# Two sides of raw-weight homes in the down projection of a hybrid decoder layer

## The chip, the core and the metric

One core of one Trainium2 chip runs the whole layer in one launch. The metric is the device time of one execution, in microseconds (us). Before the change three runs gave 1212.75, 1213.9 and 1214.02, a median of 1213.9.

## What is computed

The reference is one decoder layer on 256 tokens behind 16 meta tokens, in float32, cut here to its outline:

```python
def hybrid_layer(h, ...):
    u = rmsnorm(h, norm_mix)
    proj = u @ w_in                                    # 2048 -> 7176
    ret = head_norm(retention(q_r, k_r, v_r)) * silu(g_r)      # 8 heads
    hm = head_norm(mlstm(q_m, k_m, v_m, i, f)) * sigmoid(o_m)  # 4 heads
    h = h + concat(ret, hm) @ w_out                    # 2048 -> 2048
    u = rmsnorm(h, norm_ffn)
    gate, val = split(causal_dwconv(u @ w_up, width 3))        # 2048 -> 2 x 5632
    return h + (silu(gate) * val) @ w_down             # 5632 -> 2048
out = rmsnorm(hybrid_layer(...), norm_final)[:, 16:]
```

The change concerns the last product, `w_down`, and the memory into which all weights are loaded.

## The kernel before

**Products.** Every float32 weight block is split into a high part `whi` (ScalarE copy to fp32r, L121 or L744) and a low part `wlo` (VectorE subtraction, L123 or L746), and TensorE adds three products: high times high, high times low, low times high. A weight block is 128 x 1024 floats, 512 KB. It lands in a raw home `wraw`; there are four such homes (L116, `bufs=4`), taken in turn. The split parts have five buffers each. A raw home is free again when both halves of the split have read it.

**The stages.** Input projection and heads, output projection, then twice (for `half` in 0 and 1) 22 pairs of up-projection tiles followed by the down projection of those 22 x 256 rows. In each half the down projection runs over two pairs of column blocks (`b` = 0 and 2, L897), and in each pair over eleven steps q = 0 to 10. In half 0 the up projection ends and the down projection begins at about 720 us of the span, its second pair at about 779 us, and the up projection of half 1 at about 833 us; half 1's down projection begins at about 1089 us.

**Plain steps** (q = 0, 4, 9, 10; L919 to 924) load two blocks through `load_w`, split each and make 24 products of 128 x 512.

**Sums steps** (q = 1, 2, 3, 5, 6, 7, 8; `seven`, L812) replace the eight block products by seven of sums of blocks, 21 products of 128 x 512 in all. A step needs three raw blocks (768 KB, L821) and a fourth that was combined before and put away in DRAM, the kept piece (256 KB, L820). They lie in one of two places `left[0]` and `left[1]`, used in turn. VectorE then makes two tiles of differences, `ta` (128 x 1024, L824) and `tb` (128 x 512, L825), which take two of the four raw homes, and four splits follow: two of the raw blocks (called `hT` in the profile), `ta` and `tb`. So VectorE has per sums step four operations of 1024 columns and two of 512.

**Kept pieces** are made during the up projection (`Early`, L704). GpSimd loads raw blocks into a free place (L715), VectorE combines them (L720, L721), GpSimd writes the result to DRAM (L722). In half 0 the last two of these use `left[0]` and `left[1]`, so the first sums step's own loads into `left` wait for them: the 768 KB for L721, the kept piece (L820) for the write of L722 to end.

**The order of the work.** A scheduler of the framework orders each engine's instructions when the program is built. All plain loads, kept pieces and 768 KB loads are issued by SP, in one order; a load whose home is not free holds up the loads behind it. In half 0's first pair the homes go: step 0 takes two, steps 1, 2 and 3 take two each for `ta` and `tb`, and step 4's loads wait for the split of step 2's `ta` and `tb`.

Of the kernel before, what the change touches and what calls it, by code (L numbers as in the profile page):

```python
# [10 lines left out]
F32 = mybir.dt.float32  # L11
# [5 lines left out]
P = 128  # L17
# [16 lines left out]
W0 = GW + 2 * P  # L34
# [49 lines left out]
def trunk(ctx: ExitStack, tc: tile.TileContext, io, out: bass.AP):  # L84
    nc = tc.nc
# [5 lines left out]
    wpool = ctx.enter_context(pool("wpool", 1, side="left"))  # L91
# [20 lines left out]

    last_load = None

    def load_w(src, shape, to=None):
        nonlocal last_load  # L116
        raw = wpool.tile(shape, F32, name="wraw", bufs=4)
        last_load = nc.sync.dma_start(raw, src)
        to, n = (wpool, 5) if to in (None, wpool) else (to, None)
        hi = to.tile(shape, F32R, name="whi", bufs=n)  # L120
        nc.scalar.copy(hi, raw)  # L121
        lo = to.tile(shape, F32R, name="wlo", bufs=n)
        nc.vector.tensor_tensor(out=lo, in0=raw, in1=hi.bitcast(F32), op=ALU.subtract)  # L123
        return hi, lo
# [81 lines left out]
    with pool("sq", 1, side="right") as sqp:  # L206
        for k0, k1 in [(0, 1), (1, 2)] + [(k, k + 2) for k in range(2, KT, 2)]:
            n = k1 - k0
            nc.sync.dma_start(hT[:, k0:k1, :], io["xT"][:, k0:k1, :])
            if k0 == 0:  # L210
                nc.sync.dma_start(par[:, 0:KT], io["par"][:, 0:KT])
            raw = wpool.tile([P, 2, W0], F32, name="wraw", bufs=4)[:, :n, :]

            queue = nc.scalar if k0 < 2 else nc.sync
            load = queue.dma_start(raw, io["w0"][:, k0:k1, :])
            if k0 >= 2:
                last_load = load
# [476 lines left out]
    NQD = NHF // 2  # L694
# [29 lines left out]
    for half in range(2):  # L724
# [24 lines left out]
        for jj in range(NHF):  # L749
            j = half * NHF + jj  # L750
# [61 lines left out]
        def seven(b, q, cs, ps, first, last, after, norm):  # L812
# [8 lines left out]
            nc.sync.dma_start(raw[:, 1:4, :], io["wd7"][b // 2, half * NQD + q][:, 1:4, :])  # L821
            ta, tb = (wpool.tile([P, 2, 512], F32, name="wraw", bufs=4) for _ in range(2))

# [66 lines left out]

        def load_step(b, q, to=wpool):
            return load_w(io["wd"][b, half * NQD + q], [P, 2, 512], to)

# [3 lines left out]
        for b in (0, 2):  # L897
# [10 lines left out]
            alone = plain[-lag:] if final else []  # L908
            for q in steps:
                if q in fast:  # L910
# [8 lines left out]
                for j in range(2):  # L919
                    if j == 1 and q in alone:  # L920
                        continue
                    w = load_step(b + j, q)
                    for tt in range(2):
                        product(cs[tt, j], tt, q, w, q == plain[0], q == plain[-1 - (lag if final and (tt, j) == (1, 1) else 0)])
# [16 lines left out]
        if half == 1:  # L941
            c = 3 * 512
            ws = {}
            for n, q in enumerate(alone):
                ws[q] = load_step(3, q, more if n % 2 else wpool)
                product(cs[0, 1], 0, q, ws[q], False, q == alone[-1])
# [102 lines left out]
```

## Time and profile before

| | |
|---|---|
| median of three runs | 1213.9 us |
| the profiled execution's own time | 1212.13 us |
| its span, first to last instruction | 1210.4 us |
| TensorE busy | 1198.6 us (99%) |
| VectorE busy | 970.1 us (80%) |
| ScalarE busy | 708.5 us (59%) |
| granted TensorE clock, mean | 0.998 |
| DMA, mean over the span | 218 GB/s |

The profile covers one execution. What lies outside its span is 1.73 us. A product of 128 x 512 is shown as 0.39 us long, but the products overlap: the time of a run of them is the distance between their starts. "Idle before" in a row is the engine's idle time just ahead of the instruction, with what ended it.

### The profile page before, as it was taken

What the parts mean: (1) busy time and instruction counts of PE and PEld (TensorE: products, weight loads), DVE (VectorE), ACT (ScalarE), POOL (GpSimd) and SP (SyncE); (2) the same over time, 40 slices, a digit from 0 to 9 for tenths busy, and PEclk for the clock granted to TensorE, in tenths of its full rate; (3) what the DMA queues carried; (4) which work ended last, traced back from release to release, by engine and by line L of the source; (5) the groups of instructions that cost most, each with busy time, mean ns of one, the idle gap of its engine ahead of it and who ended that gap; (6) DMA issues with size and microseconds to landing.
All of it is one profiled execution on the core that took longest, in us unless ns stands there. A gap on an engine that the chain in (4) does not pass through costs nothing.

```text
span 1210.4 us, 22758 instructions
## 1 busy us (share of the span) xinstructions
PE 1198.6 (99%) x8956; PEld 1155.6 (95%) x8956; DVE 970.1 (80%) x1444; ACT 708.5 (59%) x963; POOL 165.1 (14%) x228
## 2 busy tenths in 40 slices
PE   9999999999999999999999999999999999999997
PEld 9999999999999999999999997788999999998886
DVE  8877778766775767789888879996798778789897
ACT  8657646656556656555555546665555555556674
POOL 0100001111110211021122210202022112100232
PEclk9999999999999999999999999999999999999999
DMA  8765555656564655766766775959777677755956
GB/s 277 265 220 160 166 189 171 199 175 189 181 193 141 208 178 176 248 220 208 246 225 209 270 268 202 261 200 272 275 252 261 216 245 239 259 177 208 286 179 185
DMA packets 83004, 263.27 MB, mean 218 GB/s; under 512 B 14672, under 2 KB 18896, under 8 KB 82768
## 3 DMA queue, kind: packets, MB, share of 16 engines
q1 hardware_dynamic: 71952, 223.85, 56.4%
q0 software_dynamic: 10368, 37.11, 10.0%
q8 instruction: 70, 1.15, 0.4%
q10 hardware_dynamic: 576, 0.85, 0.2%
q14 instruction: 38, 0.31, 0.1%
HBM read 243.42 MB, written 11.27 MB: 210 GB/s over the span
## 4 chain that ended last, share of the span: by engine, by line
PE 92%; DMA 4%; DVE 2%; issue 1%; ACT 0%; SPq 0%; DVEq 0%; POOL 0%; ACTq 0%; POOLq 0%
PE mmps L130 25%; PE mmps L131 25%; PE mmps L133 24%; PE atps L807 3%; PE atps L808 3%; PE atps L810 2%; PE mmps L842 2%; PE mmps L839 1%; PE mmps L840 1%; PE atps L842 1%; PE atps L840 1%; PE atps L839 1%; DMA wraw<-in_wd 1%; DMA hT<-in_wd 1%; DVE wlo L746 1%
## 5 line engine op out<-in xcount | busy, mean ns | idle before, releaser
L121 ACT CAST whi<-wraw 128x1024 fp32r<-128x1024 f32 x352 | 368.7, 1049 | 316.6 <-PE mmps L131 216.9
L123 DVE TENSOR_TENSOR wlo<-wraw,whi 128x1024 fp32r<-128x1024 f32 x352 | 433.1, 1232 | 71.9 <-ACT whi L121 69.6
L130 PE MATMUL mmps<-uh,whi 128*128 128x258 f32 x1408 | 346.7, 283 | 0.0
L131 PE MATMUL mmps<-ul,whi 128*128 128x258 f32 x1408 | 346.6, 283 | 0.0
L131 PEld LDWEIGHTS mmps<-ul,whi 128*128 128x128 f32 x1408 | 266.6, 189 | 0.1
L130 PEld LDWEIGHTS mmps<-uh,whi 128*128 128x128 f32 x1408 | 266.4, 189 | 0.1
L130 PE MATMUL mmps<-xh,whi 128*128 128x272 f32 (+2 forms) x864 | 219.9, 288 | 0.0
L131 PE MATMUL mmps<-xl,whi 128*128 128x272 f32 (+2 forms) x864 | 218.4, 286 | 0.0
L133 PE MATMUL mmps<-uh,wlo 128*128 128x258 f32 x1408 | 199.0, 283 | 0.0
L133 PEld LDWEIGHTS mmps<-uh,wlo 128*128 128x128 f32 x1408 | 181.3, 189 | 0.0
L131 PEld LDWEIGHTS mmps<-xl,whi 128*128 128x128 f32 x864 | 163.0, 189 | 0.0
L130 PEld LDWEIGHTS mmps<-xh,whi 128*128 128x128 f32 x864 | 162.7, 188 | 0.1
L133 PE MATMUL mmps<-xh,wlo 128*128 128x272 f32 (+2 forms) x864 | 126.8, 286 | 0.0
L133 PEld LDWEIGHTS mmps<-xh,wlo 128*128 128x128 f32 x864 | 114.4, 188 | 0.0
L633 DVE TENSOR_TENSOR cu<-mmps,rstd 128x258 f32<-128x258 f32 x88 | 37.3, 424 | 47.6 <-PE mmps L133 47.1
L746 DVE TENSOR_TENSOR wlo<-hT,whi 128x1024 fp32r<-128x1024 f32 x52 | 62.8, 1236 | 5.6 <-ACT whi L744 5.0
L744 ACT CAST whi<-hT 128x1024 fp32r<-128x1024 f32 x52 | 53.3, 1051 | 23.4 <-DMA hT<-in_wd 5.6
L131 PE MATMUL mmps<-mixl,whi 128*128 128x258 f32 x256 | 63.0, 283 | 0.0
L130 PE MATMUL mmps<-mixh,whi 128*128 128x258 f32 x256 | 62.4, 283 | 0.0
L744 ACT CAST whi<-wraw 128x1024 fp32r<-128x1024 f32 (+1 forms) x52 | 42.1, 835 | 18.5 <-DVE wraw L824 4.8
L807 PE MATMUL atps<-whi,mh 128*128 128x512 f32 (+1 forms) x132 | 50.9, 387 | 2.0 <-ACT whi L121 2.0
L746 DVE TENSOR_TENSOR wlo<-wraw,whi 128x1024 fp32r<-128x1024 f32 (+1 forms) x52 | 51.4, 1014 | 0.8 <-PE mmps L842 0.2
(276 smaller groups left out, 1704.4 us busy)
## 6 DMA issues: line engine op xcount, KB each, us to landing
wraw<-in_wu SPq DMA_DIRECT2D x176, 512.0 KB, 4.4
wraw<-in_wi SPq DMA_DIRECT2D x108, 512.0 KB, 4.2
hT<-in_wd SPq DMA_DIRECT2D x26, 768.0 KB, 4.5
wraw<-in_wd SPq DMA_DIRECT2D x36, 512.0 KB, 5.1
wraw<-in_wo SPq DMA_DIRECT2D x32, 512.0 KB, 3.8
x<-in_wd POOLq DMA_DIRECT2D x14, 768.0 KB, 7.6
hT<-in_wd POOLq DMA_DIRECT2D x12, 768.0 KB, 6.4
hn<-x POOLq DMA_DIRECT2D x27, 256.0 KB, 7.8
```

The lines of the kernel that those rows point to most:

```text
L121: nc.scalar.copy(hi, raw)
L123: nc.vector.tensor_tensor(out=lo, in0=raw, in1=hi.bitcast(F32), op=ALU.subtract)
L130: nc.tensor.matmul(ps, hi[:, k, :], xh(kk), start=kk == first, stop=False)
L131: nc.tensor.matmul(ps, hi[:, k, :], xl(kk), start=False, stop=False)
L133: nc.tensor.matmul(ps, lo[:, k, :], xh(kk), start=False, stop=kk == last)
L633: evacuated = nc.vector.tensor_tensor(out=u, in0=ps[:, :NQ], in1=rstd2, op=ALU.mult)
L744: copied = nc.scalar.copy(hi, x)
L746: return copied, nc.vector.tensor_tensor(out=lo, in0=x, in1=hi.bitcast(F32), op=ALU.subtract)
L807: nc.tensor.matmul(ps, ah[i], hi[:, i, cols], start=first and i == 0, stop=False)
L808: nc.tensor.matmul(ps, al[i], hi[:, i, cols], start=False, stop=False)
L810: nc.tensor.matmul(ps, ah[i], lo[:, i, cols], start=False, stop=last and i == 1)
L842: nc.tensor.matmul(o, sh[:, f, m, :], lo[:, i, :], start=False, stop=end)
```

## The change

The four raw homes become two sides of two, `wraw0` and `wraw1`, of the same total size. Loads outside the down projection take them in the order 0, 0, 1, 1. In the down projection `ta` and `tb` of a sums step take side 1, and plain steps take side 0, except the last one of a pair (q = 10, and of half 1's second pair the one where the index is odd), which takes side 1. The loads of a plain step that follows a sums step are asked for ahead of that sums step; the splits stay where they were. Nothing is computed otherwise.

```diff
     last_load = None
+    loads = 0
+
+    def raw_home(shape, side):
+        return wpool.tile(shape, F32, name=f"wraw{side}", bufs=2)
+
+    def load_raw(src, shape, side=None):
+
+        nonlocal last_load, loads
+        raw = raw_home(shape, loads % 4 // 2 if side is None else side)
+        loads += 1
+        last_load = nc.sync.dma_start(raw, src)
+        return raw
 
     def load_w(src, shape, to=None):
-        nonlocal last_load
-        raw = wpool.tile(shape, F32, name="wraw", bufs=4)
-        last_load = nc.sync.dma_start(raw, src)
+        return split_w(load_raw(src, shape), shape, to)
+
+    def split_w(raw, shape, to=None):
...
-            ta, tb = (wpool.tile([P, 2, 512], F32, name="wraw", bufs=4) for _ in range(2))
+            ta, tb = (raw_home([P, 2, 512], 1) for _ in range(2))
...
-        def load_step(b, q, to=wpool):
-            return load_w(io["wd"][b, half * NQD + q], [P, 2, 512], to)
+        def load_step(b, q, side):
+
+            return load_raw(io["wd"][b, half * NQD + q], [P, 2, 512], side)
+
+        def split_step(raw, to=wpool):
+            return split_w(raw, [P, 2, 512], to)
...
-            for q in steps:
+            raws = {}
+
+            def load_plain(q):
+                side = 0 if q == plain[0] or q not in steps[steps.index(fast[-1]) + 2 :] else plain.index(q) % 2
+                for j in range(1 if q in alone else 2):
+                    raws[q, j] = load_step(b + j, q, side)
+
+            for n, q in enumerate(steps):
+
+                if q in plain and (q, 0) not in raws:
+                    load_plain(q)
+                if n + 1 < len(steps) and steps[n + 1] in plain and q in fast:
+                    load_plain(steps[n + 1])
                 if q in fast:
...
-                    w = load_step(b + j, q)
+                    w = split_step(raws[q, j])
...
-                ws[q] = load_step(3, q, more if n % 2 else wpool)
+                ws[q] = split_step(load_step(3, q, n % 2), more if n % 2 else wpool)
```

How this moves the instructions, at the three places that matter. First SP, from the last up-projection loads of half 0 to the loads of step 6 of the first pair. `in_wu` are up-projection blocks, `in_wd` plain blocks, `in_wd7` the 768 KB loads, `kept0_1` the kept piece of step 1. Before:

```order
L118 DMA wraw_8982<-in_wu 128x1024
L118 DMA wraw_9039<-in_wd 128x1024
L118 DMA wraw_9057<-in_wd 128x1024
L821 DMA hT_72<-in_wd7 128x1536 x2
L820 DMA hT_72<-kept0_1_6036 128x512
L820 DMA hT_72<-kept0_2_6320 128x512
L820 DMA hT_72<-kept0_3_6612 128x512
L821 DMA hT_72<-in_wd7 128x1536
L820 DMA hT_72<-kept0_5_6904 128x512
L821 DMA hT_72<-in_wd7 128x1536
L118 DMA wraw_9204<-in_wd 128x1024
L118 DMA wraw_9222<-in_wd 128x1024
```

and with the change:

```order
L124 DMA wraw0_8982<-in_wu 128x1024
L124 DMA wraw0_9039<-in_wd 128x1024
L124 DMA wraw0_9041<-in_wd 128x1024
L124 DMA wraw0_9161<-in_wd 128x1024
L834 DMA hT_72<-in_wd7 128x1536 x2
L124 DMA wraw0_9163<-in_wd 128x1024
L833 DMA hT_72<-kept0_1_6036 128x512
L833 DMA hT_72<-kept0_2_6320 128x512
L833 DMA hT_72<-kept0_3_6612 128x512
L834 DMA hT_72<-in_wd7 128x1536
L833 DMA hT_72<-kept0_5_6904 128x512
L834 DMA hT_72<-in_wd7 128x1536
```

Step 4's two loads (9204 and 9222 before, 9161 and 9163 now) have moved from behind the loads of step 5 to both sides of the first two 768 KB loads, ahead of the kept piece of step 1; and the second load of step 0 (9057, now 9041) takes the home that `wraw_8982` had just before it.

Second VectorE, where the last two kept pieces are made and step 0's blocks are split (`wlo_9043` before and `wlo_9045` now is the split of step 0's first block, `hT_72<-hT_72` are the two operations of each kept piece). Before:

```order
L633 TENSOR_TENSOR cu_8877<-mmps_8807,rstd2_78 128x258
L123 TENSOR_TENSOR wlo_9043<-wraw_9039,whi_9041 128x1024
L720 TENSOR_TENSOR hT_72<-hT_72 128x512
L637 SCALAR_TENSOR_TENSOR vt_8879<-cu_8877,par_73,vt_8879 128x256
L721 TENSOR_TENSOR hT_72<-hT_72 128x512
L637 SCALAR_TENSOR_TENSOR vt_8879<-cu_8877,par_73,vt_8879 128x256
L123 TENSOR_TENSOR wlo_9061<-wraw_9057,whi_9059 128x1024
L720 TENSOR_TENSOR hT_72<-hT_72 128x512
```

and with the change:

```order
L646 TENSOR_TENSOR cu_8877<-mmps_8807,rstd2_78 128x258
L733 TENSOR_TENSOR hT_72<-hT_72 128x512
L135 TENSOR_TENSOR wlo_9045<-wraw0_9039,whi_9043 128x1024
L734 TENSOR_TENSOR hT_72<-hT_72 128x512
L650 SCALAR_TENSOR_TENSOR vt_8879<-cu_8877,par_73,vt_8879 128x256
L733 TENSOR_TENSOR hT_72<-hT_72 128x512
L650 SCALAR_TENSOR_TENSOR vt_8879<-cu_8877,par_73,vt_8879 128x256
L734 TENSOR_TENSOR hT_72<-hT_72 128x512
L135 TENSOR_TENSOR wlo_9061<-wraw0_9041,whi_9059 128x1024
```

The split of step 0's first block now stands between the two operations of the first kept piece.

Third VectorE a little later, from the last scaling of an up-projection tile (`cu_9021`) through step 1 and into step 2 (`wraw_9077` and `wraw_9078` are `ta` and `tb` of step 1, 9120 and 9121 those of step 2). Before:

```order
L633 TENSOR_TENSOR cu_9021<-mmps_8951,rstd2_78 128x258
L824 TENSOR_TENSOR wraw_9077<-hT_72 128x1024
L825 TENSOR_TENSOR wraw_9078<-hT_72 128x512
L637 SCALAR_TENSOR_TENSOR vt_9023<-cu_9021,par_73,vt_9023 128x256
L824 TENSOR_TENSOR wraw_9120<-hT_72 128x1024
L746 TENSOR_TENSOR wlo_9092<-hT_72,whi_9091 128x1024
L825 TENSOR_TENSOR wraw_9121<-hT_72 128x512
L637 SCALAR_TENSOR_TENSOR vt_9023<-cu_9021,par_73,vt_9023 128x256
L746 TENSOR_TENSOR wlo_9102<-wraw_9077,whi_9101 128x1024
```

and with the change:

```order
L646 TENSOR_TENSOR cu_9021<-mmps_8951,rstd2_78 128x258
L650 SCALAR_TENSOR_TENSOR vt_9023<-cu_9021,par_73,vt_9023 128x256 x2
L837 TENSOR_TENSOR wraw1_9077<-hT_72 128x1024
L781 TENSOR_TENSOR gt_9017<-gt_9017,vt_9023 128x256
L838 TENSOR_TENSOR wraw1_9078<-hT_72 128x512
L759 TENSOR_TENSOR wlo_9092<-hT_72,whi_9091 128x1024
L759 TENSOR_TENSOR wlo_9102<-wraw1_9077,whi_9101 128x1024
L759 TENSOR_TENSOR ml_9972<-gt_9017,mh_9971 128x256
L759 TENSOR_TENSOR wlo_9112<-wraw1_9078,whi_9111 128x512
L759 TENSOR_TENSOR wlo_9125<-hT_72,whi_9124 128x1024
```

Two operations of the last up-projection tile have moved ahead of step 1's `ta`, and step 2's `ta` has moved behind the splits that free its home.

## Rows read from the trace of the kernel before

**Rows 1.** The page's head and its first part: span, busy time of each engine.

```profile
span 1210.4 us, 22758 instructions
PE 1198.6 (99%) x8956; PEld 1155.6 (95%) x8956; DVE 970.1 (80%) x1444; ACT 708.5 (59%) x963; POOL 165.1 (14%) x228
```

**Rows 2.** Stretches: busy time by engine, then clock, DMA share and GB/s.

```profile
723.30:767.00 43.70, 41.57 (x180) 33.16 (x178) 42.90 (x47) 27.35 (x32) 0.00 (x0) 1.00 0.59 202
767.00:836.00 69.00, 68.96 (x307) 56.86 (x308) 62.49 (x65) 43.15 (x50) 11.45 (x13) 1.00 0.79 233
1088.00:1202.00 114.00, 114.00 (x527) 94.62 (x525) 103.41 (x113) 72.56 (x93) 24.34 (x23) 1.00 0.67 212
```

**Rows 3.** Timeline of TensorE: start, length, instruction, idle time before it.

```profile
725.70 0.39 PE L839 MATMUL atps<-whi,sh 128*128 128x512 f32 x1
...
739.26 0.73 PE L842 MATMUL mmps<-wlo,sh 128*128 128x512 f32 x2
740.76 0.50 PE L807 MATMUL atps<-whi,mh 128*128 128x512 f32 x1 [0.76 <-ACT whi L121]
...
765.14 0.62 PE L842 MATMUL mmps<-wlo,sh 128*128 128x512 f32 x2
767.04 0.50 PE L807 MATMUL atps<-whi,mh 128*128 128x512 f32 x1 [1.28 <-ACT whi L121]
...
768.76 0.39 PE L807 MATMUL atps<-whi,mh 128*128 128x512 f32 x1
```

**Rows 4.** The chain that ended last, in order of time: start, length, what.

```profile
734.29 5.27 DMA wraw<-in_wd
...
759.88 5.96 DMA wraw<-in_wd
...
771.66 1.83 PE atps L810 x8
```

**Rows 5.** The same chain, earlier: the kept piece of step 1.

```profile
704.77 6.17 DMA hT<-in_wd
...
712.95 5.21 DMA kept<-hT
718.18 5.09 DMA hT<-kept
```

**Rows 6.** Timeline of VectorE, 703 to 724 us.

```profile
703.73 0.42 DVE L768 TENSOR_TENSOR gt<-gt,vt 128x256 f32<-128x256 f32 x1
...
706.78 1.22 DVE L123 TENSOR_TENSOR wlo<-wraw,whi 128x1024 fp32r<-128x1024 f32 x1
...
710.96 0.69 DVE L720 TENSOR_TENSOR hT<-hT 128x512 f32<-128x512 f32 x1 [0.58 <-DMA hT<-in_wd]
...
711.97 0.68 DVE L721 TENSOR_TENSOR hT<-hT 128x512 f32<-128x512 f32 x1
...
723.29 1.23 DVE L824 TENSOR_TENSOR wraw<-hT 128x1024 f32<-128x1024 f32 x1 [2.48 <-DMA hT<-kept]
```

**Rows 7.** Timeline of VectorE inside the first pair, three operations in a row.

```profile
742.00 1.22 DVE L824 TENSOR_TENSOR wraw<-hT 128x1024 f32<-128x1024 f32 x1
743.14 0.69 DVE L825 TENSOR_TENSOR wraw<-hT 128x512 f32<-128x512 f32 x1
743.74 1.22 DVE L123 TENSOR_TENSOR wlo<-wraw,whi 128x1024 fp32r<-128x1024 f32 x1
```

**Rows 8.** The view of line L820, all 26 kept pieces read back: from issue to landing.

```profile
DMA to landing us min/median/max: 2.5/2.6/5.7
```

**Rows 9.** Stretches again, around the change from up to down projection.

```profile
690.00:712.50 22.50, 22.50 (x189) 22.50 (x188) 20.23 (x33) 12.24 (x17) 4.57 (x9) 1.00 0.92 351
712.50:721.50 9.00, 9.00 (x72) 8.78 (x71) 6.42 (x12) 2.98 (x5) 1.10 (x2) 1.00 0.85 264
```

**Rows 10.** Timelines of ScalarE and TensorE where half 1's up projection begins.

```profile
834.61 1.05 ACT L121 CAST whi<-wraw 128x1024 fp32r<-128x1024 f32 x1 [0.75 <-DMA wraw<-in_wu]
...
837.35 0.28 PE L130 MATMUL mmps<-uh,whi 128*128 128x258 f32 x1
```

More of the change, by code (lines that the diff above doesn't have):

```diff
@@ L211, in trunk @@
                 nc.sync.dma_start(par[:, 0:KT], io["par"][:, 0:KT])
-            raw = wpool.tile([P, 2, W0], F32, name="wraw", bufs=4)[:, :n, :]
+            raw = raw_home([P, 2, W0], loads % 4 // 2)[:, :n, :]
+            loads += 1
             queue = nc.scalar if k0 < 2 else nc.sync
```

## The prediction

> **What bounds the kernel now.** I read the page first, then the busy time of the engines by stretch, then TensorE's own timeline in the one stretch where it waits, and last the chain of waits to see what is late there. On the page TensorE is busy for 1198.6 of 1210.4 us [rows 1]. So the change can win only where TensorE waits, and lose wherever it makes it wait. By stretches it waits in one place alone: in the first pair of half 0's down projection it is busy 41.57 of 43.70 us, while the second pair and the whole of half 1's down projection show 68.96 of 69.00 and 114.00 of 114.00 [rows 2]. A change to the homes in those other stretches has nothing to take away.
>
> In the first pair the timeline gives the waits. Eight products take 1.83 us, 0.229 each [rows 4]. After the pair of products at 739.26 and another at 0.38 later the next was due at 739.83; it starts at 740.76, 0.93 late, and the wait is for ScalarE's copy of a plain block. The same at 767.04, due at 765.60: 1.44 late [rows 3]. The chain names what ScalarE waited for: a plain load asked for at 734.29 that took 5.27, and one asked for at 759.88 that took 5.96 [rows 4]. These are the first loads of steps 4 and 9, late because their homes held `ta` and `tb`. The whole pair, from the first product of step 1 at 725.70 to the point at 768.76 where step 9 goes on, holds seven times 21, 24 and 4 products, 175, which need 40.03; it takes 43.06 [rows 3]. So 3.0 us is lost, 2.4 of it in the two waits, and that is the most that can be won.
>
> **What stands behind those waits.** In the same stretch VectorE is busy 42.90 of 43.70 us [rows 2]: it works without a break from the moment the kept piece of step 1 lands, at 723.29, after an idle 2.48 [rows 6]. One 1024-column operation follows the next by 1.14, one of 512 by 0.60 [rows 7]. A sums step is four and two of them, 5.76, against 4.80 for its 21 products, so VectorE falls back 0.96 in each; a plain step gives back 5.49 less 2.28. This run of VectorE will not go away with the loads.
>
> **The change, part by part.**
>
> *The loads of steps 4 and 9.* They are now free of `ta` and `tb` and asked for up to 20 us sooner. Both waits, 0.93 and 1.44, go. What is late next is VectorE's chain. By the new order VectorE has from step 1's `ta` through step 8's `ta` 27 operations of 1024, 12 of 512 and two short ones that start 0.34 apart like the one at 703.73 [rows 6]: 30.78 + 7.20 + 0.68 = 38.66 after the piece lands. The last operation's tail is 0.08, ScalarE's copy with its start 1.10 [rows 10], and 15 products follow to the point of comparison, 3.43: together 43.3 after the landing. Before it was 768.76 - 723.29 = 45.5. So at an unchanged landing the first pair would win **2.2**, not 3.0: 0.8 comes back as a wait for step 8's `ta`, which can no longer be made ahead in a third or fourth home. The two scalings of the last up-projection tile that now stand ahead of `ta` cost nothing: they fit into the idle 2.48 ahead of it.
>
> *The landing itself.* Each 1 us by which step 1's kept piece comes later is 1 us lost, since nothing in VectorE's run is idle. The chain says how it comes: an early load asked for at 704.77, 6.17 under way; VectorE's two operations, ending the second at 712.65; the write at 712.95, 5.21; the read at 718.18, 5.09 [rows 5, 6]. Three edits touch it.
> (a) Step 0's second load now takes the home whose split ends at 708.00 [rows 6], so its 0.524 MB move into the early load's time. DMA runs at 351 GB/s there, 0.92 busy [rows 9]: 1.49 us of transfer. Nothing to 1.49 for the early load; shared evenly, 0.75.
> (b) VectorE's split of step 0's first block now stands between the two operations. From landing to write it took 2.01; now 0.60 + 1.14 + 0.68 and GpSimd's 0.30, 2.72: 0.71 more. The write is asked for at 712.95 + 0.75 + 0.71 = 714.4, and the read at 719.6.
> (c) Step 4's two loads now stand in front of the piece on SP, one ahead of the two 768 KB loads and one behind. The second waits for a split that follows the kept pieces on VectorE; that ends well before 719.6, so SP is not held up. But the bytes are ahead. The 26 pieces land in 2.6 in the median [rows 8], this one took 5.09 right behind a 768 KB load. From 714.4 on there are two loads of 0.524 MB, two of 0.786, two written pieces and the piece itself of 0.262 each: 3.41 MB. At 351 GB/s, the rate just before, that lasts until 724.1; at 264, the rate of the stretch itself [rows 9], until 727.3. Below both lies a piece that is not held up at all, 719.6 + 2.6 = 722.2; VectorE is ready for it at 722.5. Above lies the slow rate with all 1.49 of (a) instead of half, and as much again for the second load: 728.8. I take the middle of the two rates, **725.7**, since the second load and the last write overlap the ramp of the first. That is 2.4 later than 723.29.
>
> Here a rule bears on it. The Trainium skill, DMA: Bandwidth & Descriptors, section Queues, rings and completion order, says that a DMA engine works off one queue's descriptors in ring order and takes turns between queues packet by packet. By it the piece has to wait for step 4's two loads as well, which speaks against asking for them here; without it the piece could pass them and the first pair would win all of it. The trace agrees so far as the piece took 5.09 where the median is 2.6 [rows 8].
>
> *The sum.* 43.3 - 45.5 + 2.4 = +0.2 us. The profiled execution, 1212.13, becomes 1212.3. It lay 1.8 under the median, so the median becomes **1214.1**.
>
> *The rest.* Half 0's second pair and half 1 lose the lead of one step in `ta` and `tb`, 1.74 us of VectorE work; VectorE has 6.5 and 10.6 us idle there [rows 2], and I take nothing. Without that cover it is up to 1.7 in one pair. At half 1's start the second up-projection block takes a side 1 home and its load falls into third place; the third load was copied from 834.61 to 835.66 and TensorE comes to the second block at 837.35 [rows 10], 1.7 to spare: nothing. Up-projection and head stages keep the order 0, 0, 1, 1, four homes in turn as before.
>
> **The rivals.**
> 1. *The piece isn't held up* (faster). Step 4's first load fills time in which DMA is little used and the second goes around the piece; the landing stays near 722.5. For it: the 2.6 median [rows 8]. Against it: 264 GB/s and 0.85 busy in just that stretch [rows 9]. TensorE then runs at its 40.03: 3.0 less, 1210.9. It is over 0.2% faster (2.4 us, about what a measurement of this kernel can tell) if the landing comes before 723.1. Chance 0.14.
> 2. *The piece is held up for longer* (slower). The place is the same queue: both edits (a) and (c) at their upper bounds, a landing at 728.8, VectorE 5.5 later, TensorE waiting from step 1's `ta` on. For it: DMA is 0.92 busy already and this very piece took twice the median. Price +3.3, 1217.2. It decides for slower at landings after 727.9. Chance 0.12.
> 3. *A wait that takes the place of the old one elsewhere*: TensorE at half 1's start waits because the block in third place lands 2 to 3 us later than the third load did. Price 0.3 to 1.3 on top, 1214.4 to 1215.4. For it: those loads take 5 us and more behind others; against it the 1.7 to spare. Chance 0.06, and no change of side.
>
> **How the numbers follow.** The forecast, a landing between 723.1 and 727.9 and so a change between -2.4 and +2.4, has 0.68. Same is 0.76: the forecast, the third rival and 0.02 from the first, whose landing may come a little late. Faster is 0.12 and slower 0.12. The range reaches from a landing of 723.3 (-2.2, less 0.2 for the scatter of the runs) to 727.9: 1211.7 to 1216.3; beyond it lie the two outer rivals.
>
> **What would show it.** In the profile after: no idle time of TensorE ended by ScalarE's copies of plain blocks in the first pair; step 4's and step 9's loads landed long before their copies; the first VectorE operation on step 1's `ta` at about 725.7 with an idle time for the kept piece of some 3 us or more; from there VectorE without a break for some 42 us; TensorE's idle of about 3 us now ended by the copies of `ta` or by step 1's pieces. A landing near 723 with TensorE free would prove the first rival, and one past 728 the second. TensorE idle in half 1, or at the second up-projection block at about 837 us, would prove the sum incomplete.

## The result, and the profile after

The change makes the kernel slower. Six runs have a median of 1218.82 us (1216.4 to 1219.61), six of the kernel before 1213.33 (1211.98 to 1214.21). The ratio is 1.0043, 95% interval 1.003 to 1.0056: 5.2 us more, at least 3.6 and at most 6.8. The forecast was 1214.1 with a range up to 1216.3 and a chance of 0.12 for slower. It was wrong.

The profiled execution took 1217.26 us, its span 1215.5; before it was 1212.13 and 1210.4. The page's head and first part, against [rows 1]:

```profile
span 1215.5 us, 22759 instructions
PE 1201.3 (99%) x8956; PEld 1154.8 (95%) x8956; DVE 970.0 (80%) x1444; ACT 704.0 (58%) x963; POOL 172.9 (14%) x228
```

The work is the same: as many products, and VectorE is busy as long. So the 5.1 us of span are waits of TensorE. To find them I read the start of the same product in TensorE's timeline of both kernels at five places:

| product | before | after | lost since the place ahead |
|---|---|---|---|
| first of step 1, half 0 | 725.70 | 725.92 | 0.22 |
| step 0's second block, second pair | 781.57 | 782.70 | 0.91 |
| first of half 1's down projection | 1089.09 | 1091.29 | 1.07 |
| step 0's second block, last pair | 1147.47 | 1150.51 | 0.84 |
| last product | 1201.84 | 1206.96 | 2.08 |

Each pair of column blocks loses 0.8 to 2.1 us. This ledger (first, second, third and last pair, of one execution; the second entry reaches over half 1's up projection) is given for every run below. The stretches are those of [rows 2], begun at about the same places of the program (stretch, length, busy time of PE, PEld, DVE, ACT, POOL with instructions, granted clock, DMA share, GB/s):

```profile
724.74:768.14 43.40, 42.35 (x181) 33.47 (x181) 43.40 (x47) 28.57 (x33) 0.39 (x1) 1.00 0.55 184
768.14:837.14 69.00, 67.10 (x294) 54.06 (x293) 59.49 (x62) 38.37 (x44) 10.22 (x12) 1.00 0.75 223
1090.20:1206.96 116.76, 115.29 (x526) 94.17 (x525) 104.85 (x113) 71.09 (x92) 23.74 (x23) 1.00 0.63 198
```

In the first row VectorE has no idle time left, as forecast. In the second and third, where TensorE had been busy without a gap, it now stands idle for 1.9 and 1.5 us. The second row begins in step 9 of the first pair, so 1.37 of its 1.9 is a wait of that pair, at step 10.

**The first pair up to step 9** went as forecast, but for the landing's parts (below). VectorE's timeline shows the landing of the kept piece, and TensorE's the steps that the loads of steps 4 and 9 had held up [rows 3]:

```profile
724.74 1.22 DVE L837 TENSOR_TENSOR wraw<-hT 128x1024 f32<-128x1024 f32 x1 [0.76 <-DMA hT<-kept]
```

```profile
725.92 0.39 PE L852 MATMUL atps<-whi,sh 128*128 128x512 f32 x1
...
740.17 0.63 PE L855 MATMUL mmps<-wlo,sh 128*128 128x512 f32 x2
740.63 0.40 PE L820 MATMUL atps<-whi,mh 128*128 128x512 f32 x1
...
766.09 0.62 PE L855 MATMUL mmps<-wlo,sh 128*128 128x512 f32 x2
766.54 0.39 PE L820 MATMUL atps<-whi,mh 128*128 128x512 f32 x1
...
768.14 0.39 PE L820 MATMUL atps<-whi,mh 128*128 128x512 f32 x1
...
770.89 1.99 PE L823 MATMUL atps<-wlo,mh 128*128 128x512 f32 x8
774.26 0.50 PE L820 MATMUL atps<-whi,mh 128*128 128x512 f32 x1 [1.37 <-ACT whi L133]
```

The piece was asked for at 719.86 and landed at 724.72. VectorE was ready for step 1's `ta` at 723.98, after two scalings that now stand ahead of it, and waited 0.76 for the piece. Steps 4 and 9 (740.63, 766.54) start without a wait, and from step 1's first product to the point in step 9 it takes 42.22 in place of 43.06. So 0.84 is won. **Step 10** gives it back and more: its first product was due 1.83 after 770.89, at 772.72, and starts at 774.26. ScalarE's timeline says what it waited for:

```profile
773.16 1.04 ACT L133 CAST whi<-wraw 128x1024 fp32r<-128x1024 f32 x1 [5.71 <-DMA wraw<-in_wd]
```

Step 10's load is asked for only when step 8's `ta` has been split, at 766.29, and takes 6.8 us. This was so before too: with four homes in turn step 10 got the homes of step 8's `ta` and `tb`, and its load was asked for at 765.63, when that split ended, and took 5.79. Since TensorE was 1.44 late at step 9, the copy was still ready 0.79 ahead of its use: the old wait was its cover. Now the use is due 0.61 sooner, the load is asked for 0.66 later and takes 1.01 longer, and 0.79 ahead becomes 1.5 behind.

**The second pair.** TensorE starts 0.45 late at step 3 and 0.41 late at step 8, with these rows:

```profile
797.82 0.50 PE L852 MATMUL mmps<-whi,sh 128*128 128x512 f32 x1 [0.28 <-ACT whi L757]
...
823.06 0.50 PE L852 MATMUL mmps<-whi,sh 128*128 128x512 f32 x1 [0.24 <-ACT whi L757]
```

Step 4's two loads, asked for at 779.67 and 782.17, stand on SP ahead of step 3's kept piece. DMA issues of step 3 before and after (out<-in, queue, KB each, median us from issue to landing):

```profile
hT<-in_wd SPq DMA_DIRECT2D x1, 768.0 KB, 4.2
hT<-kept SPq DMA_DIRECT2D x1, 256.0 KB, 2.7
```

```profile
hT<-in_wd SPq DMA_DIRECT2D x1, 768.0 KB, 7.5
hT<-kept SPq DMA_DIRECT2D x1, 256.0 KB, 6.0
```

The piece is asked for 0.5 later than before and lands 3.9 later. By the Trainium skill, DMA: Bandwidth & Descriptors, section Queues, rings and completion order, a DMA engine consumes the descriptors of one ring in order; the trace agrees with the 2.7 that become 6.0.

**Half 1.** In the third pair TensorE waits 0.44 for step 10's loads (the first asked for at 1134.28, landed 1140.68) and 0.16 at the step 0 behind it. In the last pair VectorE has lost its lead: step 6's `ta`, made at 1172.09 before, is made at 1179.31, 7.2 later where TensorE came to the pair 3.0 late. The loads at the end that take side 1 are asked for from 1184.55 on, where before they came from 1181.29 on, and TensorE starts 0.63 and 0.80 late for their splits. TensorE's, VectorE's and GpSimd's timelines:

```profile
1195.62 0.74 PE L823 MATMUL atps<-wlo,sh 128*128 128x512 f32 x2 [0.46 <-DVE wlo L135]
...
1201.77 0.73 PE L823 MATMUL atps<-wlo,mh 128*128 128x512 f32 x2 [0.74 <-DVE wlo L135]
```

```profile
1199.43 2.28 DVE L135 TENSOR_TENSOR wlo<-wraw,whi 128x1024 fp32r<-128x1024 f32 x1
```

```profile
1199.34 1.29 POOL L664 TENSOR_TENSOR hn<-hn,gfin 128x512 f32<-128x512 f32 x1 [5.96 <-ACT junk L660]
```

The second wait isn't the load's: that had landed at 1197.56. Its split stood on VectorE behind an operation that waited for an accumulating write until 1198.80, and then took 2.28 in place of 1.22 beside GpSimd's multiplication. With 1.22 it would have ended at 1200.65, in time.

### The profile page after: what moved, and what is told of

The parts are those of the page before. It is cut to its first block, busy times and chain, and to the rows that moved or that the text cites. A ratio compares the mean times of both kernels' runs of the same rounds, so it can differ in the third digit from the quotient of the medians.

```text
span 1215.5 us, 22759 instructions
## 1 busy us (share of the span) xinstructions
PE 1201.3 (99%) x8956; PEld 1154.8 (95%) x8956; DVE 970.0 (80%) x1444; ACT 704.0 (58%) x963; POOL 172.9 (14%) x228
## 5 line engine op out<-in xcount | busy, mean ns | idle before, releaser
L820 PE MATMUL atps<-whi,mh 128*128 128x512 f32 (+1 forms) x132 | 51.1, 388 | 1.6 <-ACT whi L133 1.6
L821 PE MATMUL atps<-whi,ml 128*128 128x512 f32 (+1 forms) x132 | 50.7, 385 | 0.0
```

Of the source, the lines that this page charges most:

```text
L820: nc.tensor.matmul(ps, ah[i], hi[:, i, cols], start=first and i == 0, stop=False)
L821: nc.tensor.matmul(ps, al[i], hi[:, i, cols], start=False, stop=False)
```

## The experiments

A run's first line below is its ratio to the kernel before with the 95% interval; the changed kernel's is 1.0043 [1.003, 1.0056] throughout. Ledgers are of the profiled execution, against the profile before. Edits are against the changed kernel.

### Which pairs lose

The separate sides are kept in one pair or left out of one; elsewhere all loads and tiles take the homes in turn. The condition differs (`== (0, 0)`, `!= (0, 0)`, `!= (1, 2)`):

```diff
+        def sum_home(b):
+            nonlocal loads
+            if (half, b) == (0, 0):
+                return raw_home([P, 2, 512], 1)
+            loads += 1
+            return raw_home([P, 2, 512], (loads - 1) % 4 // 2)
...
-            ta, tb = (raw_home([P, 2, 512], 1) for _ in range(2))
+            ta, tb = (sum_home(b) for _ in range(2))
...
-                    w = split_step(raws[q, j])
+                    w = split_step(raws[q, j] if sided else load_step(b + j, q, None))
```

**Sides in the first pair alone**

> The two sides are kept in half 0's first pair alone; the other three pairs draw all four homes in turn, as the kernel before does. Theory A (each pair loses by its own homes: a plain step 10 whose loads must wait for step 8's sums, sums that can no longer be made a step ahead, a tail whose reloads wait): of the 5.1 us that the two profiled runs differ by, the first pair with its own step 10 holds 0.8 (0.7 won up to step 9, 1.5 lost at step 10), so this run is 0.8 slower than the kernel before, 0.3 to 1.5, and TensorE has no wait of over 0.3 us after the 1.5 at step 10. Theory B (the lateness is handed on: the later pairs wait because the first one has shifted their loads and pieces against one another): this run stays 3 us or more slower than before, with the waits in the later pairs where the changed kernel has them.

1.0015 [1.0001, 1.0028]; ledger 0.48, -0.01, 0.01, 0.00. In the profile the first pair loses a little and the three others lose nothing. That execution was the fastest of its twelve; by the times the loss is 0.1 to 3.4 us, against 3.6 to 6.8 for the changed kernel. So most of the loss is where I had forecast none.

**Sides everywhere but in the first pair**

> The complement: half 0's first pair draws the four homes in turn, the other three pairs have the two sides. Theory A: second pair 1.1, third pair 0.9, last pair 2.1, so 4.1 us slower than before (3.0 to 5.0), with the two old waits of 0.9 and 1.4 back in the first pair and the waits of about 0.4 in the second. Theory B: with nothing handed on from the first pair it is within 1 us of the kernel before.

1.0062 [1.004, 1.0084]; ledger 2.92, 3.56, 1.70, 1.31. The other pairs lose without the first, but the sizes are off. The first pair lost 2.92 though its homes go in turn: its kept piece landed at 725.94. And most of the second entry is this run's own doing: the 14 tiles that its first pair draws in turn shift the order 0, 0, 1, 1 by two, so half 1's first up-projection block takes side 1, is asked for behind the second and third, and makes TensorE start 2.8 late. In the changed kernel that block is on side 0. Without this wait and the first pair 3.7 are left, near the 4.1 expected. TensorE's timeline:

```profile
841.36 0.39 PE L142 MATMUL mmps<-uh,whi 128*128 128x258 f32 x1 [2.55 <-ACT whi L133]
```

**Sides everywhere but in the last pair**

> The two sides in the first three pairs, the last pair of half 1 (with the tail's reloads) in turn. Theory A: the last pair's 2.1 us go and nothing else does, so 3.0 us slower than before (2.2 to 3.8), and TensorE has no wait over 0.3 us in the last 20 us. Theory B: the tail's waits come from the lateness that it was handed, and stay: 4.5 to 5.1 us slower than before.

1.0067 [1.0048, 1.0085]; ledger 0.74, 3.26, 1.57, 2.77. I had expected the last pair's loss to go; it grew. Homes in turn did bring most of the lead back: step 6's `ta` is made at 1178.74, 6.7 later than before where TensorE came to the pair 6.1 late. But the end's reloads were asked for at 1188 to 1194 and fell beside the accumulating writes of `share` (L878 in this run). DMA issues of the end, before and in this run:

```profile
wraw<-in_wd SPq DMA_DIRECT2D x5, 512.0 KB, 4.8
hn<-x POOLq DMA_DIRECT2D x3, 256.0 KB, 4.3
```

```profile
wraw<-in_wd SPq DMA_DIRECT2D x5, 512.0 KB, 7.2
hn<-x POOLq DMA_DIRECT2D x3, 256.0 KB, 7.9
```

**The changed kernel once more, on another chip**

> The changed kernel as it is, on the chip of the next three, since the times of the last four runs scattered by more than their places explained. Theory A (loads that land with no time to spare, so that one that comes a little later is waited for): TensorE waits at the same kind of places as in the first profile (ta of steps 2, 3 and 8, step 10, the tail), 4 to 8 us slower than before in all, and the size of the waits on loads differs from the first profile by 0.5 us or more at one place at least, the second up-projection block of half 1 among the candidates (0.3 us to spare in the first profile). Theory B (a fixed price): the same waits within 0.2 us each, and 4.5 to 5.5 us slower.

A median of 1217.84 against 1212.02; ledger 1.99, 1.47, 1.25, 1.45. Most waits stand at the same steps with other sizes (2.20 at step 10 in the first pair, 0.93 at the end). Two are new, 0.80 at 779.47 and 1.06 at 1148.09, both for ScalarE's copies that empty TensorE's results, and those at step 10 of the third pair and beside GpSimd's multiplication are gone. Much of this is loads that come just in time: one execution shows where they wait, not how much each costs.

### The wait at step 10

**Step 10's loads into a home of the sums steps' raw blocks**

> The changed kernel, but step 10 of the first three pairs is loaded into the home of the next sums step's raw blocks (free as soon as step 7 is split) and no longer into the side that step 8's ta and tb hold. Theory A: its loads are asked for some 5 us sooner, so the waits at step 10 go (1.5 in the first pair, 0.9 in the third); the waits for ta in the second pair and those in the tail stay: 2.7 us slower than before (1.8 to 3.5). Rival (step 10 waits for ScalarE and VectorE, which are late behind step 9, and its load only came last): TensorE waits the same 1.5 at step 10, with its load landed long before, and the time is that of the changed kernel, 5.1 slower.

```diff
             def load_plain(q):
+                nonlocal turn
+                if q == steps[-1] and not final:
+                    raws[q, 0], raws[q, 1] = left[turn][:, 0:2, :], left[turn][:, 2:4, :]
...
```

1.0124 [1.0102, 1.0147]; ledger 7.77, 2.46, 5.19, 3.75. The wait at step 10 is gone (its loads land at 764.14 and 766.42, and its product at 774.10 starts when due), so the home was its cause. The time says nothing on its price, because a larger wait came at 783.25. Waits of TensorE (us in total, times, longest), and ScalarE's timeline:

```profile
PE atps L820 <- ACT x L967: 11.0, 2, 6.0
```

```profile
788.75 0.59 ACT L967 COPY x<-atps 128x512 f32<-128x512 f32 x1 [8.93 <-DMA hn<-x]
```

The second load of the second pair's step 0 came late now (it landed at 777.69), and in this run's order three of VectorE's four operations of `share` stood behind its split (778.87), the accumulating writes behind those, and the copies that empty TensorE's results behind the writes. One late split, four links further, is six microseconds.

**A third home for step 10's sake, and for the tiles of steps 3 and 7**

> The changed kernel, with ta and tb of steps 3 and 7 in rows 2 to 4 of x5, which are idle there, so that the sums of steps 3, 5, 7 and 8 can be made a step ahead again; step 8's stay on side 1, and so step 10's loads wait for them as before. Theory A (the sums' two homes are what TensorE waits for within the pairs): the two waits of 0.4 us in the second pair, at step 3's and step 8's ta, go, and the time from the second pair's second block to the start of half 1's up projection falls from 1.1 over the kernel before to under 0.3; the wait of 1 to 1.5 at step 10 of the first pair stays. Rival (ta is late because VectorE works in order behind splits that wait for ScalarE): the waits for ta in the second pair stay at 0.3 to 0.5 each.

```diff
+            if q in (3, 7):
+                ta, tb = x5[:, 2:4, :], x5[:, 4:5, :]
+            else:
+                ta, tb = (raw_home([P, 2, 512], 1) for _ in range(2))
```

(`x5`, L630, is in use only around a pair's end.) 1.0067 [1.0054, 1.008]; ledger 1.22, 2.08, 2.43, 4.21. The second pair still waits (0.22, 0.84, 0.54, partly at other steps), so a third home for `ta` and `tb` alone doesn't remove its loss. VectorE waits for the raw blocks themselves (waits, then timeline):

```profile
DVE x L840 <- DMA hT<-in_wd: 3.2, 2, 1.9
```

```profile
793.39 1.23 DVE L840 TENSOR_TENSOR x<-hT 128x1024 f32<-128x1024 f32 x1 [1.30 <-DMA hT<-in_wd]
```

**The same for steps 3, 6 and 8, and step 10's split behind `share`** (`q in (3, 6, 8)`; `issue_after` the last operation of `share`)

> The changed kernel with ta and tb of steps 3, 6 and 8 in x5. Side 1 is free after step 7, so step 10's loads are asked for some 4 to 5 us sooner, and the sums of a step can again be made during the step ahead of it. VectorE's split of step 10 is told to follow the last of the four operations that share out the sums. Theory A: the waits at step 10 (first and third pair) and those for ta in the second pair go; what stays is the first pair's wait for the kept piece and the tail, so 1 to 3 us slower than before, 2 to 4 faster than the changed kernel. Rival (the lateness only moves on to step 0's loads behind, since it is DMA's rate that sets them): TensorE waits over 0.7 at step 10 or at the step 0 that follows it, and no more than 1 us is won.

1.0057 [1.0045, 1.0069]; ledger -2.05, 3.07, 0.00, 2.48. The first pair wins 2.05 and the third loses nothing: with step 8's tiles out of side 1, step 10's loads were asked for at 759.57, and TensorE, 2.3 sooner there than before, doesn't wait. The second pair still lost at steps 3 and 7, behind plain loads (kept piece 6.8 us), and the program ended 12.35 after the last product instead of 8.52, since `share` and its writes came late.

### The order on SP

What puts step 4's loads ahead of the piece? Built without the two lines that ask for a plain step's loads ahead of the sums step, the program has the same order of instructions on all five engines, but for buffer numbers. So the place in the source did nothing here; the scheduler asks for a load when its home is free, and a side of its own is free sooner.

**Plain loads behind the 768 KB load of the step**

> The changed kernel with one thing moved: the plain loads that were asked for sooner (steps 4 and 9 of the first three pairs, 4, 7 and 8 of the last) are told to follow, on SP, the raw blocks of the sums step ahead of them; the homes stay as they are. VectorE's first ta of half 0 is held behind the last up-projection tile, as it stands in the changed kernel. Theory A (the order on the ring): step 4's loads stood ahead of step 3's kept piece, which took 6.0 us in the second pair where it took 2.7 before; it now lands within 3.5 us of its asking, step 3's blocks land 2 to 3.5 us sooner, the wait at step 3 (0.45) goes, step 1's kept piece in the first pair lands by 724.0, and the waits for step 10's loads (1.5 to 2.2 and 0.6 to 1.1) stay: 1 to 2.5 us faster than the changed kernel, so 2.8 to 4.3 slower than before. Theory B (the sums' two homes alone): both waits in the second pair stay at 0.4 to 0.5 and the time is the changed kernel's, 5 slower than before.

```diff
-                if n + 1 < len(steps) and steps[n + 1] in plain and q in fast:
-                    load_plain(steps[n + 1])
...
+                    if n + 1 < len(steps) and steps[n + 1] in plain:
+                        with tc.issue_after(blocks.ins):
+                            load_plain(steps[n + 1])
```

(The first `ta` is held behind the last up-projection tile, where VectorE would wait for it too soon.) 1.0042 [1.0028, 1.0056]; ledger -1.27, 0.23, 2.06, 1.61. Half 0's places behaved: step 1's piece took 3.8 (717.28 to 721.03), step 3's of the second pair 3.5, and both waits of the second pair went. Step 10's 1.06 stayed. Half 1 lost as before, and by the time the kernel is no better than the changed one.

**The same beside the changed kernel on one chip**

> The changed kernel once more, only to stand beside the next three on one chip: 4.5 to 6.5 us slower than before, as in the two timings so far (both 1.0043).

> The run in which the plain loads follow the raw blocks of the sums step ahead, beside the changed kernel on one chip. Its profile won 2.3 us up to step 9 and lost little in the second pair, but its time, 1.0042 of the kernel before, was no better than the 1.0043 that the changed kernel had on another chip. Theory A (the ring's order is a large part of the loss, and the chips differ): 1 to 3 us faster than the changed kernel here. Theory B (what is won in half 0 is waited for again in half 1, where step 10 and the tail set the time): within 0.7 us of the changed kernel, with larger waits in half 1.

The changed kernel had a median of 1218.49 and a ledger of 0.85, 1.93, 1.02, 1.96; the moved loads 1.0024 [1.0012, 1.0036], a median of 1216.93 and 0.08, -0.02, 1.18, 1.44. Issues of the second pair's step 3 with the loads moved:

```profile
wraw<-in_wd SPq DMA_DIRECT2D x2, 512.0 KB, 5.9
hT<-in_wd SPq DMA_DIRECT2D x1, 768.0 KB, 4.7
hT<-kept SPq DMA_DIRECT2D x1, 256.0 KB, 3.1
```

The piece takes 3.1 in place of 6.0, and the second pair has no wait: the ring's order is the cause of its loss. (The first pair has a new wait, 1.43 at 739.32, which is 0.41 on the other chip.) In the medians that is 1.6 us, and the runs of each kernel spread over some 4 to 6, so its price in time is a hint, not more; half 1's loss is left. In the changed kernel's profile half 1's third up-projection block, whose load falls into fourth place, makes TensorE start 0.73 late, the third rival's mechanism one block further on:

```profile
842.70 0.39 PE L142 MATMUL mmps<-uh,whi 128*128 128x258 f32 x1 [0.57 <-ACT whi L133]
```

### Mends, and a kernel faster than both

**Sides in the first pair alone, and a third home there**

> The two sides in half 0's first pair alone, with ta and tb of its steps 3, 6 and 8 in x5, and VectorE's split of step 10 behind the sharing out; the other pairs in turn as before. No load is moved on SP against the changed kernel but step 10's, which are asked for when step 7 is split. Theory A: TensorE comes to step 10 2.5 to 3.2 us sooner than in the kernel before, as in the run with the third home in all pairs, and since the later pairs lose nothing, keeps 1.8 or more of it to the end: 1.8 to 3.2 us faster than before. Rival (what the first pair wins is a wait that step 0's loads, or the sums of the second pair, would have hidden): less than 0.8 us stays.

> The run before with the loads of steps 4 and 9 told to follow the raw blocks of steps 3 and 8 on SP, and the first ta held behind the last up-projection tile. Theory A (ring order): step 1's kept piece lands 0.5 to 1.5 us sooner after its asking than in the run before, and the first pair, which is bound by VectorE from that landing on, wins as much: 0.3 to 1.2 us faster than the run before. Rival (the piece is held up by the two 768 KB loads ahead of it alone): it lands within 0.3 us as long after its asking, and the times agree within 0.3 us.

0.9999 [0.999, 1.0007], ledger -1.51, -0.02, 0.76, 0.01; and with the plain loads behind the blocks 0.9991 [0.9982, 1.0], ledger -2.38, -0.01, 0.18, 0.25. The kept piece took 5.4 and 3.8, and the write ahead of it 6.5 and 5.4: step 4's loads again. The second run's first pair wins 0.9 over the first's, as expected, and its time points the same way, though the intervals overlap. The first run reached step 10 1.9 sooner than before, short of the 2.5 to 3.2 expected, and its time missed the expected gain altogether.

**All three mends** (plain loads behind the blocks in all pairs; third home for steps 3, 6, 8 in all but the last; splits of step 10 and, in the last, of the reloads behind `share`)

> The sides in all four pairs, and three things mended: plain loads behind the raw blocks of the sums step ahead; ta and tb of steps 3, 6 and 8 in x5 in the first three pairs (so that step 10's loads are asked for when step 7 is split); VectorE's splits of step 10 and of the tail's reloads behind the sharing out. Theory A (ring order, the loads of step 10 and the lead of the sums are all that the change costs up to the last pair): no wait over 0.5 in the second pair, none over 0.5 at step 10, half 1's up projection starts 1.5 or more sooner than in the kernel before, and with what is left in the last pair the time is between 1.5 us faster and 1.5 slower than before. Theory B (something else in the sides costs, as a lower rate of DMA, or the step 0 behind): it stays 2.5 us or more slower than before, or starts half 1 later than it.

0.9992 [0.9979, 1.0005], a median of 1212.14 against 1216.93 with the loads moved alone; ledger 0.25, 1.65, 0.00, 0.04. So the change's 5.2 us are gone, with the sides kept everywhere. The places I had named were partly wrong: new waits of 1.34 and 1.12 came at 729.83 and 818.93, half 1's up projection starts about 1 later than before and not 1.5 sooner, and which mend removed the last pair's loss these runs don't separate.

**Sides in the first pair alone, mended there**

> The two sides in half 0's first pair alone, ta and tb of its step 8 in x5 (step 10's loads 4 to 5 us sooner), VectorE's split of step 10 behind the sharing out, and step 4's two loads told to follow step 1's kept piece on SP; the rest in turn as before. Theory A: the kept piece lands at 723.0 to 724.2 (724.7 in the changed kernel), TensorE reaches step 9 0.9 to 1.9 us sooner than in the kernel before, doesn't wait at step 10, and keeps that to the end: 0.8 to 2 us faster than before. Rival (the piece is late for its early load and its write, and not for the loads ahead of it): it lands within 0.4 of 724.7, and the gain is 0.5 or less.

> The version that was 0.17% faster than before, whose profiled execution was the slowest of its twelve, once more for a time on another chip and a profile nearer its median: 0.8 to 3 us faster than before, with step 10 of the first pair reached 1 to 2.5 us sooner and no waits of over 0.3 in the later pairs. If it was that chip's scatter, it is within 0.6 us of before.

```diff
+            if (half, b, q) == (0, 0, 8):
+                ta, tb = x5[:, 2:4, :], x5[:, 4:5, :]
+            else:
+                ta, tb = (sum_home(b) for _ in range(2))
...
+                first = (half, b, q) == (0, 0, 4)
+                with tc.issue_after(pieces[0, 1].ins) if first else nullcontext():
...
+                    w = split_step(raws[q, j] if sided else load_step(b + j, q, None), after=done if (half, b) == (0, 0) and q == steps[-1] else None)
```

Step 4's loads stand behind step 1's piece, step 8's tiles in the third home, step 10's split behind `share`. On two chips: 0.9983 [0.9972, 0.9995], 1209.89 against 1212.02, and 0.998 [0.9968, 0.9993], 1211.26 against 1214.50. About 2 us faster than the kernel before and 7 faster than the changed one. The second run's page and stretches:

```profile
span 1209.1 us, 22760 instructions
PE 1198.5 (99%) x8956; PEld 1155.6 (96%) x8956; DVE 969.1 (80%) x1444; ACT 709.4 (59%) x963; POOL 168.8 (14%) x228
```

```profile
722.00:764.00 42.00, 42.00 (x186) 34.44 (x185) 42.00 (x48) 28.65 (x34) 0.00 (x0) 1.00 0.61 211
764.00:833.00 69.00, 69.00 (x310) 56.91 (x309) 62.02 (x65) 41.85 (x49) 11.92 (x14) 1.00 0.75 220
```

TensorE has no gap left in half 0's down projection: the ledger is -3.00, -0.04, 0.77, 0.95, and 3.0 is what the prediction had as the most to be won. VectorE's timeline has the landing that this needs, 3.8 sooner than in the changed kernel (the piece is asked for 2.9 sooner and takes 3.96 in place of 4.86):

```profile
720.95 1.23 DVE L848 TENSOR_TENSOR wraw<-hT 128x1024 f32<-128x1024 f32 x1 [1.04 <-DMA hT<-kept]
```

The first run's profile was its slowest execution of twelve (1214.91): there the piece was asked for at 720.84 and landed at 725.43, a wait of 1.55 came at 741.18, and the ledger is 1.52, 0.48, 0.00, 0.00. So one kernel's first pair differs by 4.5 between two executions; what it is worth is said by the times.

## Why the prediction was wrong

**What bounds the kernel, and what could be won: right.** TensorE's waits stood in one place and were worth 3.0; the mended kernel won 3.00 there.

**The loads of steps 4 and 9: right.** Both waits are gone, VectorE works through, and from the landing to the point in step 9 it takes 43.42 where 43.3 was forecast. That the win falls from 3.0 to 2.2 for `ta` was right as well: TensorE starts 0.80 late at 764.60, for step 8's `ta`.

**The landing: right to 1 us, by luck in its parts.** Forecast asked for at 719.6 and landed at 725.7; measured 719.86 and 724.72. But the early load took 5.33 where it had taken 6.17, so edit (a) did not come; edit (b) did (2.76 from landing to write, 2.72 forecast). The write was asked for at 712.74, not 714.4, and took 7.11, not the 5.21 that the sum kept. The write alone accounts for the 1.45 by which the piece landed later than before; the piece itself took 4.86 where it had taken 5.09. Edit (c), step 4's loads in front, is real, on the write above all: with them behind the piece the write took 5.2 to 5.4 in six runs and the piece 3.8 to 4.6; with them in front, in nine, 6.2 to 7.1 and 4.9 to 5.9. VectorE was ready at 723.98, not 722.5, so by this order rival 1's 3.0 could not have been won in full. Rival 1 and rival 2 didn't come.

**The sum for the first pair: wrong by a term left out.** "The sum. 43.3 - 45.5 + 2.4 = +0.2 us" ends in step 9. There the kernel did better than forecast: 0.62 ahead where the sum said 0.2 behind, as the piece landed sooner. The prediction followed the loads that gain a home and not the one that still waits for `ta` and `tb`: step 10's, behind step 8's tiles in both kernels. It cost 1.54 in the first profile and 2.20 and 1.06 in two others, and with 0.84 won up to step 9, and 0.2 lost behind step 10 in pieces too small to trace, the pair lost 0.91. The old waits had covered it.

**"The rest ... and I take nothing": the step that failed.** It cost 1.07 + 0.84 + 2.08 = 4.0 of the 5.1 us. I had looked at VectorE's idle time, 6.5 and 10.6 us, and set the lost lead of 1.74 against it. An idle sum over a stretch covers nothing at the step where a load is late. In the second pair the term was the very one I had priced in the first: edit (c) holds in every pair, since the homes are the same, and there the piece came 3.9 later. That this is the cause is shown by the moved loads (6.0 to 3.1, both waits gone). In the third pair it was step 10's load again: with step 8's tiles in a third home that entry is 0.00. In the last pair the lead went (`ta` made 7 us later), the reloads were asked for 3.3 to 4.4 later with TensorE 3.0 late and took up to 1.7 longer, and the largest wait, 0.80, was a split on VectorE beside GpSimd. That the sides cause the loss of these pairs is shown (no loss there with sides in the first pair alone); how the last pair's 2.08 divide between lead, lateness from earlier pairs, the accumulating writes and GpSimd isn't, since homes in turn there didn't mend it. The prediction had named the sign: TensorE idle in half 1 would prove its sum incomplete.

**Rival 3: a matter of the execution.** In the first profile half 1's second block came 0.34 ahead of its use, not 1.7. In the changed kernel's third profile TensorE started 0.73 late at the third block, and in the run with the last pair's homes in turn 0.71 and 0.76 late at the second and third.

**The chances.** Slower by over 0.2% stood at 0.12, all of it on a landing after 727.9. It came with a landing at 724.7, by places that had no rival: step 10, and the three other pairs.

## What to carry to other kernels

Homes of its own for one class of loads made the scheduler ask for these loads sooner everywhere, ahead of what came next on the same ring, and took look-ahead from the other class: price both in each place where the homes are used, not only where the wait to be removed stands. Before a wait is counted as a gain, ask which later load it has been covering; and a load that lands with a few tenths to spare can be a wait in the next execution.

## What the runs showed of the hardware

Accumulating writes are dear neighbours: beside them in the run with the last pair's homes in turn five loads of 512 KB went from 4.8 to 7.2 us in the median, and the writes of 256 KB from 4.3 to 7.9. By the Trainium skill, DMA: Bandwidth & Descriptors, section Queues, rings and completion order, an engine takes turns between rings packet by packet; that both sides slow down agrees.

VectorE and GpSimd drew each other's operations out near the end. In the changed kernel's first profile a split on VectorE that began 0.09 after GpSimd's multiplication took 2.28 us, where it takes 1.22 by itself. In its second profile the multiplication began 0.05 after the split and took 2.33, where it takes 1.29 by itself, and the split kept its 1.22.

The clock fell after some pauses of TensorE, and not after others. In the run with step 10's loads in the sums steps' home TensorE was busy 0.41 of 6.30 us, and the granted clock was 0.50 of full speed, the 1.2 GHz level, for the next 4.7 us (stretches, columns as above):

```profile
783.00:789.30 6.30, 0.41 (x2) 0.00 (x0) 0.00 (x0) 0.55 (x1) 0.78 (x2) 0.87 1.00 209
789.30:794.00 4.70, 4.62 (x11) 3.65 (x12) 2.43 (x3) 3.97 (x6) 2.49 (x3) 0.50 0.85 149
794.00:800.00 6.00, 6.00 (x27) 4.91 (x26) 6.00 (x7) 4.05 (x5) 0.00 (x0) 0.96 0.66 205
```

That is 11 products where 20 fit at 0.229 each; from 789.38 to 794.6 TensorE fell back another 2.5 us on top of the wait. In the first run of the mended first pair the clock fell after a wait of 1.55:

```profile
735.00:739.40 4.40, 4.12 (x17) 2.66 (x15) 4.40 (x6) 1.83 (x2) 0.00 (x0) 1.00 0.64 210
739.40:741.50 2.10, 0.55 (x2) 0.30 (x2) 2.10 (x3) 1.42 (x2) 0.00 (x0) 1.00 0.14 59
741.50:745.20 3.70, 3.70 (x11) 2.89 (x10) 3.70 (x5) 3.70 (x5) 0.00 (x0) 0.58 0.64 224
```

There the products stood 0.43 apart. Longer waits brought no fall elsewhere: after 2.03 at 773.96 in the changed kernel's second profile, and after 2.55 at 841.36 in the run with sides everywhere but in the first pair, the granted clock stayed at 1.00, the 2.4 GHz level. So these rows give no rule by the length of a wait.
